# Where the modulation slabs stand in the weight stream of a three-block network

## The chip, the cores and the metric

The kernel runs on one core of one Trainium2 chip. The metric is the device time of one execution in microseconds, the lower the better.

## The reference

A sequence of 256 tokens of width 1024 goes through two layers and a third block. Each layer is an FFN, a mixer and another FFN; a vector `m` that is computed from the condition `c` shifts and scales the input of each of them and gates its output:

```python
cond = jax.nn.silu(c)
for l in range(DEPTH):
    m = (cond @ w_mod[l] + b_mod[l]).reshape(bsz, 3, 3, D_MODEL)
    x = x + 0.5 * m[:, 0, 2][:, None] * swiglu(adaln_in(x, norm_g[l, 0], m, 0), ...)
    h = adaln_in(x, norm_g[l, 1], m, 1) @ w_in[l]
    mix = mixer_ab(h, ...) if l % 2 == 0 else mixer_cd(h, ...)
    x = x + m[:, 1, 2][:, None] * (mix @ w_out[l])
    x = x + 0.5 * m[:, 2, 2][:, None] * swiglu(adaln_in(x, norm_g[l, 2], m, 2), ...)
```

`w_mod[l]` has 1024 x 9216 numbers, nine sections of 1024 columns for each layer: a shift, a scale and a gate for each of the three sublayers. mixer_ab is windowed attention beside a short gated convolution, mixer_cd is dense attention beside a long convolution by a Fourier transform. The third block has a hybrid mixer (a gated linear recurrence and latent attention), attention to a memory, and a convolved FFN; it has no modulation. All data are float32.

## The kernel before, in words

**Two kinds of slabs.** All large weights lie in memory as 417 weight slabs (`wst`) of 128 x 1024 float32, 512 KB each, in the order in which the matmuls need them. `w_mod` lies there as 144 modulation slabs (`mst`) of the same size. Both kinds go through one ring of six buffers in SBUF, `raws` (line 528), and one list, `order` (lines 552 to 561), says in what sequence. `load_job` issues one transfer after the other on SyncE's queue (line 572), each as soon as a buffer of the ring is free.

**What happens to a weight slab.** ScalarE copies it to a rounded type (`hi_job`, line 594), and VectorE subtracts that copy from the slab (`lo_job`, line 608); this gives a pair in the ring `hlr` of five pairs. Both are called its conversions. TensorE multiplies each 128 x 128 block of a pair with the input, also split in two, in three matmuls of 256 or 258 columns (`mm3`), so that the accuracy of float32 is kept. A slab holds eight blocks, 24 matmuls.

**What happens to a modulation slab.** It holds 128 columns of `w_mod`, with the 1024 inputs along the free dimension. VectorE multiplies it with the condition and sums the products, in one instruction (lines 619 to 621, `tensor_tensor_reduce`, with a read of the accumulator behind it). This is called a reduction here. `lo_job` takes the slabs of both kinds in the order of the list, so a reduction stands in the same queue as VectorE's conversions. Four of the 144 slabs go to TensorE instead (`pe_mod`). Of the last section of a sublayer all eight slabs must be done before the sublayer can use it: the shift of the second FFN of a layer for instance is needed at that FFN's first matmuls.

**What the list's sequence is.** Sixteen modulation slabs stand at the start, twelve of them ahead of the first weight slab. Then `RATES` (line 304) gives for each stretch of weight slabs how many modulation slabs follow one weight slab on average: its pairs are the number of the weight slab at which a stretch ends, and the rate.

```python
    credit += next(r for e, r in RATES if i < e)
    while credit >= 1.0 and mi < NM:
        order.append(("m", mi))
```

**The stages, by weight slab.** First layer: FFN 0 to 42 up projection, 43 to 64 down projection; mixer_ab 65 to 82 in-projection, 83 to 90 out-projection; second FFN 91 to 133 up, 134 to 155 down. Second layer: FFN 156 to 198 up, 199 to 220 down; mixer_cd 221 to 238 in-projection, 239 to 246 out-projection; second FFN 247 to 289 up, 290 to 311 down. Third block: hybrid mixer 312 to 342, attention to the memory 343 to 350, FFN 351 to 416.

**How the rest is ordered.** The program is written as some hundreds of small coroutines ("jobs"). A list scheduler (`Sched`, lines 335 to 431) runs them against a rough cost of each instruction and always takes the job that could start first on its engine, so the order on every engine is fixed when the program is built. Another list of slabs makes it order the whole program anew. All engine instructions are recorded through one helper, so the profile shows them at one line, 445.

**The start of a sublayer.** The squares of the new `x` are summed, a matmul with a column of ones gives the row sums, VectorE takes the reciprocal root of them in a chain of small operations (`rsqrt`, `TENSOR_SCALAR` and so on of 128x2), TensorE spreads it over the partitions and ScalarE copies the result (`Norm.root`, `spread`). Only then can the results of a slab's matmuls be scaled (`evict`), which gives their bank of PSUM back; there are three such banks (`mmr`), so TensorE can do three slabs' worth of up-projection matmuls before it needs the first of them again. In the layers' FFNs and mixers the shift is two more columns of the input (258 instead of 256).

**The ends of the mixers.** The out-projection multiplies the mixer's outputs with `w_out`. The last outputs are split in two on ScalarE and VectorE as the input is (`split`), and the out-projection's first sums wait for them: in mixer_ab for the last channel block of the convolution, in mixer_cd for the long convolution.

Of the kernel before, what the change touches and what calls it, by code (L numbers as in the profile page):

```python
# [300 lines left out]

PHASE = 8

RATES = [(43, 0.55), (65, 0.7), (91, 0.5), (156, 0.31), (199, 0.5), (221, 0.75), (247, 0.4), (10 ** 6, 0.2)]
STAGES = (65, 91, 156, 221, 247, 312, 343, 351)

TUNE = {}
# [169 lines left out]
def _body(tc, ins, out, ctx, dbg=None):  # L477
# [76 lines left out]
    for i in range(NW):  # L554
        if i:
            order.append(("w", i))
        credit += next(r for e, r in RATES if i < e)
        while credit >= 1.0 and mi < NM:
# [1786 lines left out]
```

## Time and profile before

| what | us |
|---|---|
| three timed runs | 1431.0, 1426.72, 1430.66 |
| median | 1430.66 |
| profiled execution, whole | 1425.9 |
| its span, first to last instruction | 1424.0 |
| TensorE busy | 1375.6 |
| VectorE busy | 1141.8 |
| ScalarE busy | 778.2 |
| mean granted clock of TensorE | 0.984 |

The profile shows one execution. Its span is 1.9 us shorter than that execution's own time, and this execution is 4.8 us faster than the median of the timed runs. Times in the trace's views count from the span's start. TensorE's clock has two levels, 2.4 GHz (1.00 in the column PEclk) and 1.2 GHz; a window that shows about 0.5 was at the lower one throughout. By the trace the stages begin about here: FFN 55, mixer_ab 248, its out-projection 328, second FFN 354 (down projection 481), second layer's FFN 543 (down projection 669), mixer_cd 730, its out-projection 814, second FFN 851, hybrid mixer 1049, attention to the memory 1190, last FFN 1232.

In the timeline rows the first number is the start, the second the time until the group's last instruction ends, `x` the number of instructions, and the bracket the engine's idle time before the group and the engine whose result ended it. `CUSTOM_DVE_ANT_0` of 128x1024 is a reduction, `TENSOR_TENSOR` of 128x1024 is VectorE's conversion.

### The profile page before, as it was taken

What the parts mean: (1) busy time and instruction counts of PE and PEld (TensorE: products, weight loads), DVE (VectorE), ACT (ScalarE), POOL (GpSimd) and SP (SyncE); (2) the same over time, 40 slices, a digit from 0 to 9 for tenths busy, and PEclk for the clock granted to TensorE, in tenths of its full rate; (3) what the DMA queues carried; (4) which work ended last, traced back from release to release, by engine and by line L of the source; (5) the groups of instructions that cost most, each with busy time, mean ns of one, the idle gap of its engine ahead of it and who ended that gap; (6) DMA issues with size and microseconds to landing.
All of it is one profiled execution on the core that took longest, in us unless ns stands there. A gap on an engine that the chain in (4) does not pass through costs nothing.

```text
span 1424.0 us, 26962 instructions
## 1 busy us (share of the span) xinstructions
PE 1375.6 (97%) x10726; PEld 1292.5 (91%) x10726; DVE 1141.8 (80%) x2183; ACT 778.2 (55%) x1434; POOL 40.9 (3%) x44
## 2 busy tenths in 40 slices
PE   5899999999999999999999999999999999999998
PEld 1499999878999999999998789999998779899998
DVE  5788788796888777888979879986577878799962
ACT  2365554474555544555447646655455765576642
POOL 5200000000000000000000001000000000000000
PEclk9999999999999999999999999999998999899999
DMA  8678889754787776888974447676643244366671
GB/s 296 220 252 315 290 311 326 241 160 152 248 264 249 239 246 226 299 272 279 343 283 152 158 146 231 221 253 184 192 143 107 72 130 138 90 184 186 193 228 54
DMA packets 84655, 305.25 MB, mean 214 GB/s; under 512 B 9515, under 2 KB 11147, under 8 KB 84274
## 3 DMA queue, kind: packets, MB, share of 16 engines
q1 hardware_dynamic: 83250, 299.31, 64.5%
q0 software_dynamic: 1280, 4.22, 0.9%
q8 instruction: 84, 1.38, 0.4%
q14 instruction: 41, 0.34, 0.1%
HBM read 302.43 MB, written 1.06 MB: 213 GB/s over the span
## 4 chain that ended last, share of the span: by engine, by line
PE 84%; DVE 7%; ACT 5%; DMA 1%; POOL 1%; issue 1%; SPq 0%; ACTq 0%; DVEq 0%; POOLq 0%
PE u L445 84%; DVE u L445 7%; ACT u L445 4%; POOL u L445 1%; DMA u<-wst 1%; DMA u<-x 1%; ACT L445 0%; SPq L572 0%; POOL u L2151 0%; ACTq L445 0%; DVEq L445 0%; DVE u L1655 0%; DVE u L1159 0%; DVE u L1656 0%; DVEq L1159 0%
## 5 line engine op out<-in xcount | busy, mean ns | idle before, releaser
L445 PE MATMUL u<-u,u 128*128 128x258 f32 (+7 forms) x10724 | 1374.5, 292 | 44.7 <-ACT u L445 24.2
L445 PEld LDWEIGHTS u<-u,u 128*128 128x128 f32 (+3 forms) x10724 | 1292.2, 189 | 126.1 <-issue 50.3
L445 ACT ACTIVATE u<-u 128x1024 fp32r<-128x1024 f32 (+6 forms) x1001 | 603.1, 632 | 534.0 <-PE u L445 311.3
L445 DVE TENSOR_TENSOR u<-u,u 128x1024 fp32r<-128x1024 f32 (+5 forms) x1065 | 734.0, 721 | 181.0 <-ACT u L445 91.9
L445 DVE SCALAR_TENSOR_TENSOR u<-u,u,u 128x256 f32<-128x256 f32 (+2 forms) x393 | 185.6, 481 | 65.2 <-PE u L445 34.2
L445 ACT ACTIVATE u<-u,u 128x256 f32<-128x256 f32 (+2 forms) x323 | 165.3, 523 | 85.6 <-DVE u L445 61.0
L445 DVE CUSTOM_DVE_ANT_0 u<-u,u,u 128x1024 f32<-128x1024 f32 x140 | 179.9, 1287 | 3.8 <-DMA u<-mst 3.7
L445 DVE SCALAR_TENSOR_TENSOR u<-u,u 128x2 f32<-128x2 f32 (+5 forms) x127 | 32.5, 261 | 13.3 <-ACT u L445 5.6
L445 ACT ACTIVATE u<-u,u,u 128x256 f32<-128x256 f32 (+1 forms) x43 | 23.8, 564 | 8.3 <-DVE u L445 5.7
L445 DVE TENSOR_SCALAR u<-u,u 128x256 f32<-128x256 f32 (+1 forms) x80 | 25.8, 370 | 1.6 <-ACT u L445 0.8
L445 DVE TENSOR_SCALAR u<-u 128x2 f32<-128x2 f32 (+9 forms) x82 | 14.9, 184 | 7.2 <-PE u L445 3.7
L445 POOL TENSOR_TENSOR u<-u,u 128x256 f32<-128x256 f32 (+1 forms) x10 | 14.5, 1448 | 12.3 <-ACT u L445 11.9
L445 DVE TENSOR_REDUCE u<-u 128x2 f32<-128x512 f32 x20 | 13.3, 683 | 1.9 <-PE u L445 1.9
L445 ACT ACT_TABLE_LOAD x11 | 14.1, 1283 | 0.9 <-PEq L2322 0.7
L1338 POOL DMA_DIRECT2D u<-rope x1 | 0.5, 548 | 480.0 <-PE u L445 480.0
L445 POOL TENSOR_SCALAR u<-u 64x256 f32<-64x256 f32 (+2 forms) x12 | 12.7, 1055 | 24.5 <-DVE u L445 18.4
L445 DVE DVE_READ_ACCUMULATOR2_ANT u<- 128x1 f32 x156 | 12.7, 82 | 0.0
L445 ACT ACTIVATION_READ_ACCUMULATOR u<-u,u,u 128x1 f32 x40 | 8.2, 205 | 0.0
L445 DVE TENSOR_TENSOR u<-u 128x2 f32<-128x2 f32 (+5 forms) x36 | 6.7, 189 | 0.6
L1153 POOL DMA_DIRECT2D u<-sel x1 | 0.6, 578 | 192.9 <-DMA u<-mst 192.9
L445 DVE CUSTOM_DVE_ANT_0 u<-u,u 128x256 f32<-128x256 f32 x16 | 6.0, 420 | 0.0
L445 DVE TENSOR_TENSOR_SCAN u<-u,u 128x256 f32<-128x256 f32 x8 | 5.4, 680 | 0.0
(35 smaller groups left out, 25.8 us busy)
## 6 DMA issues: line engine op xcount, KB each, us to landing
u<-wst SPq DMA_DIRECT2D x417, 512.0 KB, 4.5
u<-mst SPq DMA_DIRECT2D x144, 512.0 KB, 4.8
u<-u POOLq DMA_DIRECT2D x1, 1536.0 KB, 10.8
u<-x SPq DMA_DIRECT2D x1, 1024.0 KB, 8.2
u<-mem SPq DMA_DIRECT2D x1, 1024.0 KB
u<-lruw POOLq DMA_DIRECT2D x2, 512.0 KB, 4.3
out<-u SPq DMA_DIRECT2D x8, 128.0 KB, 3.3
u<-decay SPq DMA_DIRECT2D x1, 512.0 KB, 8.3
```

The lines of the kernel that those rows point to most:

```text
L445: r = f(*args, **kw)
L1153: nc.gpsimd.dma_start(sel, ins["sel6"][:8, :4 * P])
L1338: nc.gpsimd.dma_start(rope, ins["rope"])
```

## The change

`RATES` gets new numbers and more stretches. In the two in-projections (65 to 82 and 221 to 238) the rate is now 0.

```diff
-RATES = [(43, 0.55), (65, 0.7), (91, 0.5), (156, 0.31), (199, 0.5), (221, 0.75), (247, 0.4), (10 ** 6, 0.2)]
+
+RATES = [(43, 0.63), (65, 0.75), (83, 0.0), (91, 0.6), (134, 0.42), (156, 0.7), (199, 0.45), (221, 0.75), (239, 0.0),
+         (247, 0.3), (10 ** 6, 0.2)]
```

Modulation slabs in each stretch of weight slabs:

| weight slabs | stage | before | changed |
|---|---|---|---|
| 0 to 42 | FFN, up | 23 | 27 |
| 43 to 64 | FFN, down | 16 | 16 |
| 65 to 82 | mixer_ab, in | 9 | 0 |
| 83 to 90 | mixer_ab, out | 4 | 5 |
| 91 to 133 | second FFN, up | 13 | 18 |
| 134 to 155 | second FFN, down | 7 | 15 |
| 156 to 198 | second layer, FFN, up | 21 | 20 |
| 199 to 220 | FFN, down | 17 | 16 |
| 221 to 238 | mixer_cd, in | 7 | 0 |
| 239 to 246 | mixer_cd, out | 3 | 3 |
| 247 to 289 | second FFN, up | 8 | 8 |

The last modulation slab follows weight slab 283 before and 286 now. The last slab that the second FFN of the first layer needs at its start follows weight slab 82 before and 90 now; that FFN begins with weight slab 91.

How the orders differ is shown at three places. In the rows, numbers behind `u_` name buffers: `u_75` to `u_80` are the ring `raws`, `u_81` to `u_90` the pairs of `hlr` (the even ones are written by VectorE), `u_70` holds the modulation of the first layer, `u_142` the condition, `u_127` to `u_134` are the banks of PSUM, `u_67` is `x`. A reduction is two rows, `ISA u_7n,u_70<-...` and the read of its accumulator, `ISA u_70 128x1`. The line numbers of the changed file are larger by two.

VectorE at the end of mixer_ab: the last convolution (`u_91`), the split of it (`TENSOR_TENSOR u_2378<-u_91` or `u_2384<-u_91`, for which TensorE waits) and the conversion of weight slab 87 (`u_86`). Before:

```order
L445 SCALAR_TENSOR_TENSOR u_91<-u_2396,u_64,u_91 128x256
L445 SCALAR_TENSOR_TENSOR u_121<-u_70,u_63 128x8
L445 SCALAR_TENSOR_TENSOR u_91<-u_95,u_119,u_91 128x256
L445 ISA u_77,u_70<-u_77,u_142,u_63 128x1024
L445 ISA u_70 128x1
L445 TENSOR_TENSOR u_2378<-u_91,u_2377 128x256
L445 TENSOR_TENSOR u_86<-u_78,u_85 128x1024
```

Changed:

```order
L447 SCALAR_TENSOR_TENSOR u_91<-u_2402,u_64,u_91 128x256
L447 SCALAR_TENSOR_TENSOR u_121<-u_70,u_63 128x8
L447 SCALAR_TENSOR_TENSOR u_91<-u_95,u_119,u_91 128x256
L447 TENSOR_TENSOR u_86<-u_75,u_85 128x1024
L447 TENSOR_TENSOR u_2384<-u_91,u_2383 128x256
L447 ISA u_79,u_70<-u_79,u_142,u_63 128x1024
L447 ISA u_70 128x1
```

The conversion of slab 87 has moved ahead of the split, and the reduction behind it.

VectorE at the entry of the first layer's second FFN: the conversions of weight slabs 93 and 94 (`u_88` and `u_90`), the chain of the reciprocal root (from the `TENSOR_SCALAR` that reads bank `u_134`) and the reductions near them. Before:

```order
L445 TENSOR_TENSOR u_88<-u_79,u_87 128x1024
L445 TENSOR_TENSOR u_92<-u_92,u_101 128x256
L445 TENSOR_TENSOR u_90<-u_80,u_89 128x1024
L445 TENSOR_SCALAR u_103<-u_134 128x2
L445 TENSOR_SCALAR u_126<-u_103 128x2
L445 TENSOR_TENSOR u_122<-u_126 128x2
L445 TENSOR_TENSOR u_122<-u_122,u_103 128x2
L445 SCALAR_TENSOR_TENSOR u_103<-u_122 128x2
L445 SCALAR_TENSOR_TENSOR u_103<-u_103,u_122 128x2 x2
L445 SCALAR_TENSOR_TENSOR u_126<-u_103,u_126 128x2
L445 ISA u_76,u_70<-u_76,u_142,u_63 128x1024
L445 ISA u_70 128x1
```

Changed:

```order
L447 SCALAR_TENSOR_TENSOR u_69<-u_67,u_121,u_68 128x256
L447 ISA u_76,u_70<-u_76,u_142,u_63 128x1024
L447 ISA u_70 128x1
L447 TENSOR_TENSOR u_88<-u_77,u_87 128x1024
L447 TENSOR_TENSOR u_90<-u_78,u_89 128x1024
L447 TENSOR_TENSOR u_92<-u_92,u_100 128x256
L447 ISA u_75,u_70<-u_75,u_142,u_63 128x1024
L447 ISA u_70 128x1
L447 TENSOR_SCALAR u_123<-u_134 128x2
L447 TENSOR_SCALAR u_122<-u_123 128x2
L447 TENSOR_TENSOR u_124<-u_122 128x2
L447 TENSOR_TENSOR u_124<-u_124,u_123 128x2
```

Before, one reduction stands behind the chain. Now two stand ahead of it, and none directly behind it (the next row after the chain is the conversion of slab 95).

TensorE in the hybrid mixer: the query roots (`u_66` against squares in `u_91` to `u_102`, 128x8, twelve of them), rotations (`u_10868,u_66`), scores of the attention (`u_10882,u_10881`) and between them the matmuls of a slab (`u_127` to `u_129`). Before, from the ninth of the query roots on:

```order
L445 MATMUL u_131<-u_66,u_102 128x8
L445 MATMUL u_131<-u_66,u_94 128x8
L445 MATMUL u_131<-u_66,u_92 128x8
L445 MATMUL u_131<-u_66,u_98 128x8
L445 MATMUL u_128<-u_68,u_87 128x256
L445 MATMUL u_128<-u_69,u_87 128x256
L445 MATMUL u_128<-u_68,u_88 128x256
L445 MATMUL u_133<-u_10868,u_66 128x256
L445 MATMUL u_128<-u_68,u_87 128x256
L445 MATMUL u_128<-u_69,u_87 128x256
L445 MATMUL u_128<-u_68,u_88 128x256
L445 MATMUL u_130<-u_10869,u_66 128x256
```

Changed, up to the first two of them:

```order
L447 MATMUL u_129<-u_10895,u_85 128x256
L447 MATMUL u_129<-u_10896,u_85 128x256
L447 MATMUL u_129<-u_10895,u_86 128x256
L447 MATMUL u_130<-u_10868,u_66 128x256
L447 MATMUL u_129<-u_10895,u_85 128x256
L447 MATMUL u_129<-u_10896,u_85 128x256
L447 MATMUL u_129<-u_10895,u_86 128x256
L447 MATMUL u_131<-u_10882,u_10881 128x256 x2
L447 MATMUL u_128<-u_68,u_87 128x256
L447 MATMUL u_128<-u_69,u_87 128x256
L447 MATMUL u_128<-u_68,u_88 128x256
L447 MATMUL u_133<-u_66,u_100 128x8
```

The query roots stood ahead of the first of these rotations and now stand behind it and behind the first scores. Elsewhere in this stage rows have changed places in the same manner; their number is the same.

## Rows read from the trace of the kernel before

**Rows 1.** The page: its first line, and its line of busy times.
```profile
span 1424.0 us, 26962 instructions
...
PE 1375.6 (97%) x10726; PEld 1292.5 (91%) x10726; DVE 1141.8 (80%) x2183; ACT 778.2 (55%) x1434; POOL 40.9 (3%) x44
```

**Rows 2.** Windows by stage: window, its length, busy time of PE, PEld, DVE, ACT, POOL; PEclk, DMA share, GB/s.
```profile
247.70:327.50 79.80, 77.84 (x579) 66.19 (x578) 66.40 (x182) 45.48 (x114) 2.08 (x3) 1.00 0.63 202
...
354.10:481.20 127.10, 124.75 (x1042) 124.33 (x1041) 107.26 (x176) 70.68 (x132) 0.00 (x0) 1.00 0.77 249
...
481.20:542.80 61.60, 61.60 (x523) 61.60 (x522) 44.84 (x63) 30.54 (x42) 0.00 (x0) 1.00 0.78 248
...
668.50:730.00 61.50, 61.50 (x522) 61.50 (x521) 55.47 (x81) 30.55 (x42) 0.00 (x0) 1.00 0.93 330
...
730.00:814.20 84.20, 81.78 (x599) 69.56 (x599) 72.07 (x179) 54.72 (x122) 1.60 (x3) 1.00 0.53 177
```

**Rows 3.** Windows: a full FFN stretch, one FFN's start, three stretches at low clock.
```profile
680.00:720.00 40.00, 40.00 (x341) 40.00 (x340) 36.50 (x53) 19.44 (x25) 0.00 (x0) 1.00 0.96 342
...
332.20:335.60 3.40, 3.40 (x19) 3.40 (x18) 0.00 (x0) 0.00 (x0) 0.00 (x0) 0.53 0.78 263
...
354.00:359.00 5.00, 3.07 (x26) 2.86 (x25) 5.00 (x12) 2.58 (x5) 0.00 (x0) 1.00 0.70 203
...
827.10:830.50 3.40, 3.40 (x12) 2.81 (x11) 1.03 (x3) 0.42 (x1) 0.00 (x0) 0.54 0.38 143
...
1089.90:1100.20 10.30, 10.30 (x28) 6.85 (x29) 4.08 (x14) 0.67 (x2) 0.00 (x0) 0.51 0.18 51
```

**Rows 4.** The page's groups of instructions: the reductions of the modulation slabs.
```profile
L445 DVE CUSTOM_DVE_ANT_0 u<-u,u,u 128x1024 f32<-128x1024 f32 x140 | 179.9, 1287 | 3.8 <-DMA u<-mst 3.7
```

**Rows 5.** Timeline of TensorE, holes in brackets: mixer_ab (four rows), mixer_cd (three).
```profile
312.47 0.65 PE L445 MATMUL u<-u,u 128*64 128x256 f32 x2 [0.49 <-ACT u L445]
...
313.40 1.31 PE L445 MATMUL u<-u,u 128*64 128x256 f32 x6 [0.29 <-ACT u L445]
...
329.97 0.39 PE L445 MATMUL u<-u,u 128*128 128x256 f32 x1 [1.05 <-ACT u L445]
...
331.06 1.83 PE L445 MATMUL u<-u,u 128*128 128x256 f32 x12 [0.71 <-DVE u L445]
...
780.66 7.86 PE L445 MATMUL u<-u,u 128*128 128x128 f32 x54 [0.56 <-ACT u L445]
...
789.31 1.40 PE L445 MATMUL u<-u,u 128*128 128x128 f32 x10 [0.80 <-ACT u L445]
...
826.15 5.13 PE L445 MATMUL u<-u,u 128*128 128x256 f32 x16 [1.77 <-ACT u L445]
```

**Rows 6.** Timeline of VectorE: the ends of mixer_ab and mixer_cd (two rows each).
```profile
329.38 1.28 DVE L445 CUSTOM_DVE_ANT_0 u<-u,u,u 128x1024 f32<-128x1024 f32 x1
...
330.58 1.55 DVE L445 TENSOR_TENSOR u<-u,u 128x256 fp32r<-128x256 f32 x2
...
823.57 1.22 DVE L445 TENSOR_TENSOR u<-u,u 128x1024 fp32r<-128x1024 f32 x1
...
824.71 0.48 DVE L445 SCALAR_TENSOR_TENSOR u<-u,u,u 128x256 f32<-128x256 f32 x1
```

**Rows 7.** Timeline of VectorE, then TensorE: entry of the first layer's second FFN.
```profile
361.39 0.36 DVE L445 TENSOR_SCALAR u<-u 128x2 f32<-128x2 f32 x2
...
362.84 1.28 DVE L445 CUSTOM_DVE_ANT_0 u<-u,u,u 128x1024 f32<-128x1024 f32 x1
...
364.05 1.22 DVE L445 TENSOR_TENSOR u<-u,u 128x1024 fp32r<-128x1024 f32 x1
...
365.65 1.09 DVE L445 TENSOR_TENSOR u<-u,u 128x256 f32<-128x256 f32 x3 [0.39 <-PE u L445]
...
356.57 9.70 PE L445 MATMUL u<-u,u 128*128 128x258 f32 x79 [1.93 <-DVE u L445]
...
366.69 5.54 PE L445 MATMUL u<-u,u 128*128 128x258 f32 x44 [0.42 <-ACT u L445]
```

## The prediction

> **What bounds the kernel now.** First the page's busy times: TensorE is busy in 1375.6 of 1424.0 us, VectorE in 1141.8 [rows 1]. The kernel is a stream of matmuls, and only what shortens that stream or opens a hole in it moves the time. A share over the whole span does not tell what VectorE's work is worth in one stage, so the windows by stage come next [rows 2]. In the FFN stages TensorE works without a break: in the down projection of the first layer's second FFN (481.2 to 542.8) it is busy 61.60 of 61.60 us, with VectorE at 44.84. In the down projection after that (668.5 to 730.0) it is again busy 61.50 of 61.50, although VectorE is at 55.47 and the transfers at 0.93 of the DMA engines. In the in-projections of the two mixers TensorE is busy 77.84 of 79.80 and 81.78 of 84.20 us, VectorE 66.40 and 72.07. Third, the timeline of TensorE in the mixers gives every place where it stood: four small holes in the middle (0.49, 0.29, 0.56, 0.80, in all 2.14 us) and one hole at the end of each in-projection, 1.05 + 0.71 us in mixer_ab and 1.77 us in mixer_cd, in all 3.53 us [rows 5]. Behind each of those two end holes the granted clock is about 0.53 for 3.40 us, the lower of the two levels (1.2 instead of 2.4 GHz) [rows 3]; the lost half of such a stretch is 3.40 x 0.47 = 1.6 us, so 3.2 for both. Everything that a freer VectorE could give back in the mixers is therefore at most 2.14 + 3.53 + 3.2 = 8.9 us, 0.6% of the run.
>
> **What is taken out and what is put in.** The new rates take 9 modulation slabs out of the in-projection of mixer_ab and 7 out of that of mixer_cd; they put 4 more into the first FFN's up projection, 5 and 8 into the up and down projections of the first layer's second FFN, and one or two either way elsewhere. The number of slabs, transfers and reductions stays. On SP's queue the 17 weight slabs that follow the first of mixer_ab are now issued one after the other; the DMA engines are at 0.63 and 0.53 there [rows 2], so no transfer was late that could now come earlier. POOL issues none of them. One modulation slab costs VectorE one reduction of 1287 ns [rows 4]; from its start to the start of what follows it is 1.21 us (362.84 to 364.05, its read of the accumulator included) [rows 7]. So 9 x 1.21 = 10.9 and 7 x 1.21 = 8.5 us of VectorE's work leave the in-projections. That is cover time, not path: what counts are the holes.
>
> **FFN streams: 0.** The fullest FFN stretch after the change takes one slab in at 0.70 per weight slab (it was 0.31 there). The trace of before already has a stretch at 0.75: from 680 to 720 us TensorE is busy 40.00 of 40.00 us with VectorE at 36.50 and the DMA engines at 0.96, 342 GB/s [rows 3]. By work, 8 more reductions bring the stretch from 481.2 to 542.8 to 44.84 + 8 x 1.21 = 54.5 us, still below the 55.47 that the other one carries without a hole [rows 2]. In the up projection from 354.1 to 481.2, 5 more make 107.26 + 6.1 = 113.3 of 127.1. The cover is the spare ring of converted weights; if it were gone, each slab would cost its 1.21 us, but nothing in these windows says that it is near.
>
> **Middle of the mixers: -1.1.** The four holes of 2.14 us [rows 5] all end with ScalarE, which has no work of the modulation itself; VectorE's reductions can only delay what ScalarE waits for. Between all of it (-2.14) and none of it (0) I take half, as nothing in the rows places a reduction in each of these chains.
>
> **Ends of the mixers: -0.1.** Here the order decides. In mixer_ab the hole of 0.71 us waits for a split of the last convolution's output on VectorE, which starts at 330.58, behind a reduction that started at 329.38 [rows 6]. In the changed order the reduction stands behind the split, but the conversion of the next weight slab has moved ahead of it in its place. A conversion takes 1.14 to 1.2 us from start to start (823.57 to 824.71) where the reduction took 1.20 [rows 6], so some 0.1 us is gained. In mixer_cd the reduction and the conversion ahead of the last output stand in the changed order too, in the other sequence: 0. The bounds are 0 and the whole 3.53 us, with the 3.2 us of clock; I stay near 0 because the rows of the order are plain.
>
> **Entry of the second FFN: +1.8.** The first reciprocal root of that FFN is computed on VectorE (a chain of small operations, 361.39 to 362.84), and the results of the first three weight slabs can be scaled, and their PSUM banks given back, only behind it. TensorE fills those banks from 356.57 to 366.27 and then stands 0.42 us until 366.69 [rows 7]. Before, two conversions stand ahead of the chain and one reduction right behind it. In the changed order two reductions stand ahead of the chain and none directly behind. That is 2 x 1.21 = 2.4 us later for the chain. Of this the reduction that has gone from behind the chain gives back at most 1.21 and at least nothing: before the first scaling at 365.65 VectorE had idled already 0.39 us [rows 7], so it was not the reduction alone that held it. So the cost lies between 1.2 and 2.4 us; I take 1.8. The same entry in the other FFNs has no reduction ahead of the chain that was not hidden already, and costs nothing. The hole would become 0.4 + 1.8 = 2.2 us, in the size of the 1.77 us behind which the clock fell, but also of the 1.93 us at 356.57 [rows 7] behind which the clock stayed at 1.00 [rows 3]. One more fall would cost 1.6 us, which the range holds.
>
> **The rest: 0.** The list scheduler lays the whole program anew, so the hybrid mixer, which holds no modulation slab, is in another order too. The matmuls are the same in number; the price is unknown, and I take 0 with bounds from the neighbouring row: from 1089.9 to 1100.2 the clock is 0.51 for 10.30 us, that is 5.0 us lost [rows 3]. One such stretch more or less is -5 or +5.
>
> **Sum.** -1.1 - 0.1 + 1.8 + 0 = +0.6 us. On the profiled execution's 1425.9 us (the span of 1424.0 and 1.9 around it) this makes 1426.5. The three timed runs have a median of 1430.66, 4.8 above the profiled one; the same on the new sum gives **1431.3 us**. A measurement of this kernel tells about 0.3%, 4.3 us, from no change, so my forecast is no change.
>
> **Rivals.**
> *The mixers are VectorE's (faster).* If the end holes and all middle holes go, and the clock with them stays up, the gain is the whole 8.9 us, less 1.8 at the second FFN: 1430.7 - 7.1 = 1423.6. For it: VectorE is busy 72.07 of 84.20 us in mixer_cd, and 8.5 us of that leave. Against it: TensorE stands there for less than 2% of the time, and the end holes keep an operation of the same length ahead. The Trainium skill (Perfetto Trace Analysis, Identifying the Most-Contended Engine) says that matmul busy time is a bad measure and that the busy time of weight loads should be used. By it the mixers look open: weight loads are busy 66.19 of 79.80 and 69.56 of 84.20 us [rows 2], no more than VectorE, and the rival would be likely. I hold against it that a record of TensorE's hole, not its load queue, shows a wait, and that the holes add up to 5.7 us only. Chance 0.18.
>
> *The hybrid mixer loses a half-speed stretch (faster).* Its order changes: the small matmuls of the query roots move behind the first rows that they had preceded. If the stretch from 1089.9 goes, the time is 1431.3 - 5.0 = 1426.3. Nothing but the changed order speaks for it. Chance 0.08.
>
> *The hybrid mixer gains one (slower).* The same new order may leave TensorE with one more stretch of thin matmuls (one column group of 8 each) around which the clock falls for 10.30 us: 1431.3 + 5.0 = 1436.3. It decides from one added stretch on; a short one of 3.40 us (+1.6) leaves the time within 0.3%. For it: the stage has its own long stretch already, and its TensorE work is thin. Against it: the number of these matmuls is unchanged. The Trainium skill (TensorE: Matmul & The Clock Gate, What's actually happening) says that the throttled state is the default and that activity releases it; by it a stage with thin work is where an added fall is to be looked for. The trace agrees as far as it goes: the 10.30 us at 0.51 hold only 28 matmuls [rows 3]. Chance 0.20.
>
> *The change does not do what it says.* The in-projections hold no modulation slab any more, but the out-projections still take 5 and 3, and those stand next to the end holes. If what matters are only those, the time stays where it was, 1430.7. Chance 0.08; it is no change as well.
>
> **The numbers.** Forecast 0.46, change without effect 0.08: no change 0.54. Faster 0.18 + 0.08 = 0.26, slower 0.20. The range reaches from 1421.5 (the first rival without the 1.8 us at the second FFN, 1421.8) to 1437 (the slower rival, 1436.3).
>
> **What would show it.** Right: the hole in front of the fourth weight slab of the second FFN (before at 366.69) grows to about 2 us; the hole before the last output of both mixers is still over 1 us and the clock still falls behind it; the windows of both FFN down projections show TensorE busy without a break. Wrong: end holes below 0.5 us and the mixers' windows shorter by 3 us or more each (first rival), a hybrid mixer that is longer or shorter by 3 us or more (the others), or TensorE idle in the down projection of the second FFN.

## The result and the profile after

| | before | changed |
|---|---|---|
| median of four runs each, same chip | 1428.69 | 1448.69 |
| lowest and highest | 1424.42, 1431.0 | 1444.15, 1450.22 |
| ratio, 95% interval | | 1.014 [1.0114, 1.0166] |
| profiled execution: span | 1424.0 | 1442.4 |
| its mean granted clock | 0.984 | 0.974 |

The change makes the kernel slower by 20 us. The forecast was no change, and the time lies above the range. The page of the changed kernel, with the first line, the line of busy times and the clock by slices:

```profile
span 1442.4 us, 26979 instructions
...
PE 1386.9 (96%) x10726; PEld 1299.0 (90%) x10726; DVE 1146.1 (79%) x2183; ACT 778.0 (54%) x1434; POOL 39.3 (3%) x44
...
PEclk9899999899999999999999999999997899999999
```

The numbers of matmuls, of VectorE's and of ScalarE's instructions are those of before [rows 1]; TensorE is busy 11.3 us longer with the same work, and idle 7.1 us longer. More busy time for the same matmuls is time at the lower clock.

To place the 18.4 us, the time of the first matmul of each weight slab was taken in both traces and the difference followed along the program. It grows at four places and shrinks at one:

| stretch of weight slabs | grows by, us |
|---|---|
| mixer_ab, 65 to 91 | +4.75 |
| entry of the first layer's second FFN, 91 to 94 | +0.56 |
| mixer_cd, 221 to 247 | -1.77 |
| entry of the second layer's second FFN, 247 to 250 | +8.83 |
| hybrid mixer, 312 to 343 | +6.08 |
| all the rest, the FFN streams among it | 0.0 |

The windows of the changed kernel, in the columns of [rows 2]:

```profile
247.93:331.50 83.57, 82.15 (x578) 69.06 (x577) 58.41 (x168) 45.40 (x114) 2.08 (x3) 0.94 0.44 139
...
278.05:288.29 10.24, 10.24 (x38) 6.72 (x38) 4.49 (x19) 0.41 (x1) 0.00 (x0) 0.50 0.17 53
...
486.75:548.30 61.55, 61.55 (x523) 61.55 (x521) 55.10 (x81) 30.23 (x41) 0.00 (x0) 1.00 0.94 323
...
735.60:818.70 83.10, 81.33 (x599) 69.28 (x597) 66.25 (x167) 54.38 (x123) 1.61 (x3) 1.00 0.40 131
...
861.73:868.56 6.83, 4.60 (x21) 4.60 (x22) 5.40 (x18) 0.51 (x1) 0.00 (x0) 0.50 0.25 86
...
1051.30:1208.80 157.50, 152.48 (x968) 126.26 (x968) 120.86 (x313) 92.39 (x186) 1.66 (x3) 0.90 0.33 103
...
1097.25:1107.49 10.24, 10.24 (x30) 7.27 (x30) 6.08 (x12) 3.68 (x7) 0.00 (x0) 0.50 0.16 52
...
1110.90:1131.38 20.48, 20.48 (x76) 13.49 (x75) 17.14 (x44) 5.60 (x10) 0.00 (x0) 0.50 0.16 51
```

The in-projections hold no modulation slab any more, as the diff says: VectorE is busy 58.41 instead of 66.40 us in mixer_ab's in-projection and 66.25 instead of 72.07 in mixer_cd's, and the down projection that took eight slabs more runs without a break, 61.55 of 61.55 us [rows 2]. But mixer_ab has got a half-speed stretch of 10.24 us that was not there, in which the profile shows TensorE busy without a gap; that is 10.24 x 0.50 = 5.1 us. The hybrid mixer, with the same 968 matmuls, has two long half-speed stretches, 10.24 and 20.48 us, where before it had one of 10.30 [rows 3]. Its window of before, for comparison:

```profile
1038.90:1190.30 151.40, 145.99 (x968) 123.57 (x967) 120.25 (x316) 93.56 (x188) 1.66 (x3) 0.93 0.35 108
```

Over the whole stage the clock cost 151.40 x 0.07 = 10.6 us before and 157.50 x 0.10 = 15.8 us now, so 5.2 of the 6.08 us are clock.

The largest single piece is the entry of the second layer's second FFN. The timeline of the changed kernel there, VectorE (four rows), TensorE (three) and POOL (one):

```profile
855.29 0.16 DVE L447 TENSOR_TENSOR u<-u,u 128x16 fp32r<-128x16 f32 x1
...
862.88 0.29 DVE L447 CAST u<-u 128x256 f32<-128x256 int32 x1 [7.43 <-issue]
...
864.08 1.22 DVE L447 TENSOR_TENSOR u<-u,u 128x1024 fp32r<-128x1024 f32 x1
...
865.22 0.36 DVE L447 TENSOR_SCALAR u<-u 128x2 f32<-128x2 f32 x2
...
855.51 1.94 PE L447 MATMUL u<-u,u 128*128 128x258 f32 x14 [0.60 <-DVE u L447]
...
863.96 10.10 PE L447 MATMUL u<-u,u 128*128 128x1 f32 x65 [6.51 <-DVE u L447]
...
874.48 1.71 PE L447 MATMUL u<-u,u 128*128 128x258 f32 x12 [0.42 <-ACT u L447]
...
855.09 0.54 POOL L2166 DMA_DIRECT2D u<-pos  x1 [117.45 <-DVE u L447]
```

VectorE stands 7.43 us in front of a CAST. This instruction turns the token positions into floats, for the rotation tables of the hybrid mixer (the job `tables`, line 2169 of the changed file), and nothing in this FFN needs it. "issue" means that the view names no releaser. The chain of waits shows the same stretch:

```profile
855.09 0.28 DMA u<-pos
855.37 0.08 DVE u L447
855.45 7.43 issue
862.88 1.03 DVE u L447 x3
```

The releaser is found by adding: POOL issues the transfer of the positions at 855.09, and the list of DMA issues gives the time until it has landed as its last number:

```profile
u<-pos POOLq DMA_DIRECT2D x1, 128.0 KB, 7.7
```

855.09 + 7.7 = 862.79, and the CAST starts at 862.88. Behind it on VectorE are queued the conversions that feed TensorE (864.08) and the chain of the root (865.22), so TensorE stands 6.51 us and the clock is at half speed for 6.83 us. The timeline of the kernel before at this entry, VectorE and POOL:

```profile
858.06 0.55 DVE L445 SCALAR_TENSOR_TENSOR u<-u,u 128x2 f32<-128x2 f32 x3
858.55 0.29 DVE L445 CAST u<-u 128x256 f32<-128x256 int32 x1
...
850.77 0.54 POOL L2164 DMA_DIRECT2D u<-pos  x1 [118.43 <-PE u L445]
```

There the same CAST stood behind the conversions, the chain of the root and a reduction. The list of DMA issues of before gives this transfer 6.3 us:

```profile
u<-pos POOLq DMA_DIRECT2D x1, 128.0 KB, 6.3
```

So the positions were there at 850.77 + 6.3 = 857.07, and the CAST, at 858.55, waited for nothing. The scheduler gives POOL's transfers no duration in its cost model, so the two places look alike to it.

### The profile page after: what moved, and what is told of

It reads as the page before. It is cut to its first block, busy times and chain, and to the rows that moved or that the text cites. A ratio compares the mean times of both kernels' runs of the same rounds, so it can differ in the third digit from the quotient of the medians.

```text
span 1442.4 us, 26979 instructions
## 1 busy us (share of the span) xinstructions
PE 1386.9 (96%) x10726; PEld 1299.0 (90%) x10726; DVE 1146.1 (79%) x2183; ACT 778.0 (54%) x1434; POOL 39.3 (3%) x44
## 4 chain that ended last, share of the span: by engine, by line
PE 86%; DVE 6%; ACT 3%; issue 1%; DMA 1%; POOL 1%; SPq 0%; ACTq 0%; DVEq 0%; POOLq 0%
PE u L447 86%; DVE u L447 6%; ACT u L447 3%; POOL u L447 1%; DMA u<-wst 1%; DMA u<-x 1%; SPq L574 0%; ACT L447 0%; POOL u L2153 0%; DMA u<-pos 0%; ACTq L447 0%; DVEq L447 0%; DVE u L1657 0%; DVE u L1161 0%; DVE u L1658 0%
## 5 line engine op out<-in xcount | busy, mean ns | idle before, releaser
L447 PE MATMUL u<-u,u 128*128 128x256 f32 (+6 forms) x10724 | 1385.9, 294 | 51.8 <-ACT u L447 28.7
L447 PEld LDWEIGHTS u<-u,u 128*128 128x128 f32 (+2 forms) x10724 | 1298.7, 190 | 138.0 <-issue 57.5
L447 ACT ACTIVATE u<-u 128x1024 fp32r<-128x1024 f32 (+5 forms) x1001 | 604.6, 632 | 566.3 <-PE u L447 348.8
L447 DVE TENSOR_TENSOR u<-u,u 128x1024 fp32r<-128x1024 f32 (+4 forms) x1065 | 736.4, 722 | 183.1 <-ACT u L447 90.1
L447 ACT ACTIVATE u<-u,u,u 128x256 f32<-128x256 f32 (+1 forms) x43 | 23.9, 566 | 7.9 <-DVE u L447 6.4
L447 DVE RECIPROCAL u<-u 128x4 f32<-128x4 f32 (+2 forms) x17 | 3.0, 175 | 5.0 <-ACT u L447 4.7
(35 smaller groups left out, 28.8 us busy)
```

Source lines behind the costliest of these rows:

```text
L447: r = f(*args, **kw)
```

## The experiments

The theory after this reading: it is not the slabs' places that cost, but the order in which the list scheduler laid the rest anew. The rival: the slabs themselves (more reductions elsewhere, other lulls in VectorE's work) bring the loss. To part the two, the scheduler's choice was replaced by a recorded list of jobs. Only the reductions still go by the scheduler's rule, ahead of the next job of the list where their key is lower. All experiments but after_2 contain this:

```diff
 def run(self, main):
...
-            j = best[1]
+            nxt = next((j for j in self.ready if pos < len(SEQ) and j.key == SEQ[pos] and not self.is_mod(j)), None)
+            if nxt is not None:
+                if mod is not None and self.key_of(mod) < self.key_of(nxt):
+                    j = mod
+                else:
+                    j = nxt
+                    pos += 1
```

In the diffs below `order_of` is such a recorded list, and the other names say how it was edited; the kernels hold the finished lists. Each was timed beside the kernel before (64 runs over the three calls, median 1426.83, 1418.57 to 1433.85). "Lost" is the span times (1 - mean granted clock), averaged over the runs; it is about what the lower clock cost, since a stretch at half speed loses half its length where TensorE is busy all through it. "Rest" is the mean time without it, that is work at full speed and waits.

| kernel | median (runs) | ratio, 95% interval | lost | rest |
|---|---|---|---|---|
| before | 1426.83 (64) | | 25.3 | 1402.1 |
| changed, with after_2 | 1447.3 (10) | 1.014 and 1.013 | 38.5 | 1408.6 |
| move_only | 1422.12 (10) | 0.9979 [0.9951, 1.0006] | 25.7 with the next | 1400.4 with the next |
| move_only_2 | 1429.32 (12) | 1.0004 [0.9981, 1.0028] | | |
| order_only | 1439.96 (4) | 1.0085 [1.006, 1.011] | 28.8 | 1410.8 |
| cast_later | 1436.52 (7) | 1.007 [1.0046, 1.0093] | 30.8 | 1406.0 |
| ab_old_order | 1443.4 (5) | 1.0093 [1.0055, 1.0132] | 31.1 | 1410.5 |
| hybrid_old_order | 1439.29 (4) | 1.0077 [1.005, 1.0105] | 33.1 | 1406.3 |
| both_apart | 1430.0 (12) | 1.0013 [0.9996, 1.0031] | 22.5 | 1407.0 |
| after_mended | 1432.6 (10) | 1.0038 [1.0016, 1.0059] | 25.1 | 1408.6 |
| positions_early | 1436.53 (7) | 1.0075 [1.0045, 1.0105] | 33.9 | 1403.5 |
| hybrid_apart | 1426.47 (12) | 0.9992 [0.9966, 1.0017] | 23.2 | 1403.2 |

**The slabs alone: move_only.** The new rates, with the jobs in before's order; TensorE's and ScalarE's orders are then exactly those of before.

```diff
+SEQ = order_of(before)
```

> The new list of slabs, but every other job in the order of the kernel before: TensorE's, ScalarE's and POOL's instructions stand exactly as before, on VectorE only the reductions have moved. Theory (the re-sorted order costs the time, not the slabs' places): 1424 to 1432 us, TensorE's clock about 0.984, no wait of some 7 us at the start of the second layer's second FFN. Rival (the slabs themselves cost it, by work that the FFN stages cannot take): 1443 us or more, with TensorE idle in the FFN stages.

Measured: 0.9979 [0.9951, 1.0006]; the median lies 2 us below the range of the theory. The same slabs in the same places cost nothing. By slabs, its profile is 2.48 us shorter than before's in mixer_ab and 1.13 in mixer_cd, and the entries of the second FFNs are where they were. Of the 2.48 us 1.7 are a fall of the clock that before has behind the end of mixer_ab (332.2 to 335.6 [rows 3]) and this profile has not.

**The order alone: order_only.** The old rates, with the jobs in the changed kernel's order.

```diff
-RATES = [(43, 0.63), (65, 0.75), (83, 0.0), (91, 0.6), (134, 0.42), (156, 0.7), (199, 0.45), (221, 0.75), (239, 0.0),
-         (247, 0.3), (10 ** 6, 0.2)]
+RATES = [(43, 0.55), (65, 0.7), (91, 0.5), (156, 0.31), (199, 0.5), (221, 0.75), (247, 0.4), (10 ** 6, 0.2)]
+SEQ = order_of(changed)
```

> The old list of slabs, but every other job in the order of the changed kernel. Theory (order): 1443 to 1452 us, with the half-speed stretch in mixer_ab near 278 us, the wait of about 6.5 us near 864 us and some 30 us at half speed in the hybrid mixer. Rival (slabs): 1425 to 1432 us.

Measured: 1.0085 [1.006, 1.011], 1439.96 us, between the two ranges. The order without the change's slabs costs 0.9%, some six tenths of the loss. Its profile is 5.47 us longer in the hybrid mixer, but the entry costs only 2.83, because the positions landed after 4.2 us here and VectorE stood 1.95 us. Mixer_ab does not get the half-speed stretch near 278 us (it is 2.43 us longer all the same, with 6.83 us at half speed at its end where before had 3.41); the window there:

```profile
273.00:290.00 17.00, 17.00 (x114) 13.22 (x113) 13.54 (x49) 7.64 (x16) 0.00 (x0) 1.00 0.66 212
```

So the theory "order alone" holds for two of the three places, and some 7 us of the loss come only where the new order and the new slabs meet.

**The CAST moved back: cast_later.** The changed kernel with the job `tables` 60 places later.

```diff
-SEQ = order_of(changed)
+SEQ = moved_back(order_of(changed), "tables", 60)
```

> The changed kernel with the jobs of the rotation tables (first of them the cast of the positions) 60 places later in the order from the second layer's second FFN on; TensorE's order is untouched. Theory: the 6.5 us in which TensorE stands near 864 us is VectorE waiting for the positions' transfer, so it goes and the time falls by 6 to 9 us, to 1440 to 1443. Rival (the wait at that entry comes from the slabs or from the shift of the new FFN): the hole stays over 4 us and the time at 1446 to 1450.

Measured: 1.007, 1436.52 us, some 4 us below the range. The entry costs 2.42 instead of 8.83 us, and 1.53 more for a fall of the clock behind it. What remains is a neighbour in the list: the norm of the memory now stands ahead of the first scalings and waits for a transfer of 1 MB of its own, on ScalarE, for which VectorE then waits 3.87 us. ScalarE's row:

```profile
865.46 0.51 ACT L523 ACTIVATE u<-u,u 128x256 fp32r<-128x256 f32 x1 [7.59 <-DMA u<-mem]
```

The hybrid mixer too came out shorter here (+2.16), with the same matmuls in the same order, so the ratio alone does not show what the CAST is worth.

**mixer_ab in the old order: ab_old_order.** Only mixer_ab's jobs stand as before.

```diff
+SEQ = replaced(order_of(changed), "mixer_ab", order_of(before))
```

> The changed kernel with the jobs of mixer_ab in the order of before and all else in the changed order. Theory: the half-speed stretch of 10.24 us in mixer_ab comes from the closer packing of the small matmuls of the queries, so it goes and the time falls by 4 to 6 us, to 1443 to 1445. Rival (it comes from VectorE or the transfers with no slab in the mixer): the stretch stays, 1447 to 1450.

Measured: 1.0093, 1443.4 us. That number lies in the theory's range by luck: the half-speed stretch in mixer_ab is there all the same, and what was gained was gained elsewhere (the hybrid mixer is only 0.27 us longer than before's). The windows of ab_old_order and of move_only, which have mixer_ab in the same order:

```profile
277.44:291.10 13.66, 13.66 (x47) 8.79 (x46) 7.29 (x28) 1.72 (x3) 0.00 (x0) 0.50 0.15 57
```

```profile
273.45:282.30 8.85, 8.85 (x45) 5.28 (x45) 5.73 (x17) 2.22 (x4) 0.00 (x0) 1.00 0.36 113
```

TensorE is busy without a gap in both, and one runs at 0.50, the other at 1.00. The order within mixer_ab does not decide it. That theory falls. Up to the end of mixer_ab TensorE has the same matmuls in the same order in these two kernels, so the difference does not lie in TensorE's order at all; where it lies was not found.

**More slab matmuls between the small ones: both_apart.** What stands in the long ones of these stretches are matmuls with few rows of contraction (8 to 64 of 128), mostly with three full ones of a slab between them. This kernel is move_only with six instead of three in mixer_ab and the hybrid mixer.

```diff
+SEQ = spaced(order_of(before), ["mixer_ab", "hybrid_mixer"], 6)
```

> As move_only, but in mixer_ab the four spreads and first scores of the queries, and in the hybrid mixer the six spreads of the key roots and the first scores, have six matmuls of a weight slab between one and the next instead of three. Theory (the half-speed stretches follow small matmuls that stand too close): no half-speed stretch near 275 us in any run, the one of 10.24 us in the hybrid mixer (1084 to 1096) gone, 1413 to 1420 us, and no longer runs at both 1418 and 1430. Rival (the stretches come from somewhere else, or the later scores only open another hole): the clock as in move_only, 1420 to 1432.

Measured: 1.0013 [0.9996, 1.0031], 1430.0 us: the rival's range, 10 us above the theory's. Its windows in mixer_ab and in the hybrid mixer, at 1.00 and 0.95:

```profile
270.00:290.00 20.00, 20.00 (x137) 16.15 (x137) 12.04 (x47) 9.27 (x19) 0.00 (x0) 1.00 0.35 116
...
1075.00:1110.00 35.00, 34.89 (x216) 28.19 (x215) 23.64 (x68) 21.76 (x37) 0.00 (x0) 0.95 0.33 106
```

In this profile the clock stays up; hybrid_apart below shows that it need not. And the chains that the small matmuls belong to end later, and TensorE runs out of slab work before they do. The timeline of TensorE shows a new hole in mixer_ab (before, the largest in its middle was 0.49 us [rows 5]):

```profile
314.93 0.65 PE L523 MATMUL u<-u,u 128*64 128x256 f32 x2 [2.91 <-ACT u L523]
```

Lost falls by 2.8 us against before, which the scatter of the runs hardly tells from nothing; the rest grows by 4.9. What the clock gives is paid back in waits.

**All three mended: after_mended.** The changed kernel's order with `tables` and the memory's norm later and six slab matmuls in both places.

```diff
+SEQ = spaced(moved_back(order_of(changed), {"tables": 75, "memory_norm": 40}), ["mixer_ab", "hybrid_mixer"], 6)
```

> The changed kernel in its own order but for three places: the tables and the norm of the memory later at the entry of the second layer's second FFN, and six instead of three matmuls of a slab between the small matmuls of mixer_ab and of the hybrid mixer. Theory (these three places make up the loss of 20 us): 1424 to 1432 us, no hole over 3 us at that entry and less than 16 us lost to the low clock. Rival (the loss is spread over the program, or lies with the slabs): 1438 or more.

Measured: 1.0038 [1.0016, 1.0059], 1432.6 us, just above the theory's range. The entry costs 0.01 us, and lost is down to 25.1, before's level, but not below the 16 that the theory asked for. Mixer_ab keeps its clock where six profiles of the changed slabs and order had lost it:

```profile
277.00:290.00 13.00, 12.67 (x89) 10.07 (x89) 8.81 (x36) 6.49 (x21) 0.00 (x0) 1.00 0.14 46
```

It is still 1.99 us longer than before's, by a new hole of 1.94 us and a short fall. So about 14 of the 20 us go, and what stays is in the rest (1408.6 against 1402.1), as in both_apart.

**The hybrid mixer in the old order: hybrid_old_order.** The changed kernel up to there, then before's order.

```diff
+SEQ = until(order_of(changed), "hybrid_mixer") + since(order_of(before), "hybrid_mixer")
```

> The changed kernel, with the order of before from the hybrid mixer on. Theory (order): the hybrid mixer is 4 to 6 us shorter than in the changed kernel, 1442 to 1445 us, the hole near 864 us stays. Rival (the hybrid mixer is slow by the phase of the clock alone): as the changed kernel, 1447 to 1450, or spread over both.

Measured: 1.0077 against 1.014 and 1.013, by these ratios 8 to 9 us less; 1439.29 us is 3 us below the theory's range. In its profile the stage is 0.65 us shorter than before's and 6.7 shorter than the changed kernel's, the entry costs 8.98 us, and mixer_cd, which has the changed kernel's order, is at half speed for 10.24 us near 766 us, where no other profile of that order is. Of the half-speed stretches in the hybrid mixer one is long:

```profile
1110.30:1120.50 10.20, 10.20 (x29) 7.11 (x27) 5.09 (x14) 1.14 (x3) 0.00 (x0) 0.50 0.29 93
```

**A repeat of move_only: move_only_2.** Its first result was 0.2% below before, at the edge of its interval.

> The kernel of move_only once more, to tell its gain from the scatter. If moving the slabs alone pays: 1418 to 1424 in most runs and a ratio below 0.998 with its interval below 1. If it does not: ratio between 0.998 and 1.002. The profile shows a second time whether mixer_ab falls to half speed with the same order.

Measured: 1.0004 [0.9981, 1.0028]. No gain. Mixer_ab has no half-speed stretch in this profile either and is 2.41 us shorter than before's; mixer_cd is as long as before's (+0.07), with a half-speed stretch of 6.83 us near 761 us. The 22 runs together have a median of 1426.80 beside 1426.83, a lost share equal to before's and a rest that is 1.7 us lower.

**A repeat of the change: after_2**, beside the next kernel.

> The changed kernel once more, for its scatter. If the half-speed stretches of its first profile (mixer_ab, 20 us in the hybrid mixer) belong to its order, they stand in this profile too and the runs lie at 1444 to 1450. If they depend on where an execution's clock happens to stand, some of them are missing here and single runs reach 1435 or less. The wait of about 6.5 us for the positions stands in either case.

Measured: 1.013 [1.01, 1.016]. Both long stretches and the wait are there again. The hybrid mixer is at half speed even longer here, with the same program:

```profile
1101.95:1139.50 37.55, 37.55 (x136) 27.79 (x135) 25.67 (x62) 11.83 (x19) 0.00 (x0) 0.50 0.20 57
```

At the entry of the first layer's second FFN this profile shows what the first had not, a fall of the clock behind the hole (TensorE's row, then the window):

```profile
374.96 20.29 PE L447 MATMUL u<-u,u 128*128 128x258 f32 x155 [2.79 <-ACT u L447]
...
374.91:378.32 3.41, 3.36 (x15) 3.36 (x16) 2.80 (x4) 2.73 (x6) 0.00 (x0) 0.50 0.69 220
```

**The positions early: positions_early.** The changed kernel in its own order, the CAST where it was; only the transfer that it waits for is issued earlier, in mixer_cd, into a buffer that is free until the tables are made.

```diff
+    posi = rope2[:, 1].bitcast(I32)
...
+            nc.gpsimd.dma_start(posi, bass.AP(ins["pos"].tensor, ins["pos"].offset, [[0, P], [1, T]]))
...
-        posi = tl(sp, [P, T], I32)
-        nc.gpsimd.dma_start(posi, bass.AP(ins["pos"].tensor, ins["pos"].offset, [[0, P], [1, T]]))
```

> The changed kernel in its own order on every engine, but POOL issues the transfer of the positions in mixer_cd, over 100 us before VectorE's cast reads them. Theory (TensorE's hole near 864 us is the cast waiting for that transfer): the hole of 6.5 us goes, and the half-speed stretch of 6.83 us behind it with it, 8 to 10 us less than the changed kernel in the same call. Rival (VectorE is held there by the slabs or the shift): the hole stays.

Measured: 1436.53 beside 1445.95 for after_2 on the same chip, 9.4 us less (medians of 7 and 6 runs; by the means 9.1, with a 95% interval of about 4 to 14). The timeline of this kernel at the entry, VectorE, TensorE, POOL:

```profile
859.27 0.29 DVE L523 CAST u<-u 128x256 f32<-128x256 int32 x1
...
859.42 9.73 PE L523 MATMUL u<-u,u 128*128 128x258 f32 x79 [0.61 <-DVE u L523]
...
870.17 10.07 PE L523 MATMUL u<-u,u 128*128 128x258 f32 x82 [1.03 <-ACT u L523]
...
741.53 0.55 POOL L1421 DMA_DIRECT2D u<-pos  x1
```

The CAST stands in the same place and waits for nothing, the hole of 6.51 us is gone, and the entry takes 0.63 us more than before's instead of 8.83. This settles that the wait was for the positions' transfer. By slabs the entry is 8.0 us shorter than in after_2. The hybrid mixer of this profile is the worst of all:

```profile
1091.45:1132.41 40.96, 40.96 (x145) 29.75 (x144) 26.59 (x65) 12.51 (x20) 0.00 (x0) 0.50 0.19 59
```

**The hybrid mixer alone apart: hybrid_apart.** both_apart without its part in mixer_ab.

```diff
+SEQ = spaced(order_of(before), ["hybrid_mixer"], 6)
```

> As move_only, with six matmuls of a slab between the small matmuls of the hybrid mixer alone (in the kernel with both, mixer_ab had lost about 5 us and the hybrid mixer had gained about 2). If that holds: 2 us below move_only, 1421 to 1425, ratio 0.996 to 0.999. If the scatter of the clock made it: ratio 0.999 to 1.003.

Measured: 0.9992 [0.9966, 1.0017], 1426.47 us: the reading by scatter. Its hybrid mixer has the list of both_apart, job by job, and is 1.86 us longer than before's where that one was 1.77 shorter; a long half-speed stretch has come back a little later in the stage:

```profile
1122.85:1133.09 10.24, 9.76 (x36) 6.05 (x36) 8.46 (x20) 2.65 (x6) 0.00 (x0) 0.50 0.18 53
```

So six matmuls between the small ones do not hold the clock up there. Over the runs lost is some 2 us lower than before's, within their scatter, and the rest 1.1 higher; of both_apart's 4.9 us of waits, then, 3.8 come from mixer_ab. No version was found that beats the kernel before by more than its measurement can tell.

**The loss, put together.** By the means, 38.5 - 25.3 = 13.2 us of it are clock, and 1408.6 - 1402.1 = 6.5 us are waits; 5.1 of these go in positions_early (1403.5). By place:

- The CAST's wait with the fall behind it: 9.4 us. The cause is shown by positions_early.
- mixer_ab's half-speed stretch: the stage is 4.75 to 5.62 us longer. This is shown as a place, not as a cause: it fell in all six profiles that have the changed kernel's slabs, its order ahead of mixer_ab and three slab matmuls between the small ones, and in none of the others; which detail counts stays open.
- The hybrid mixer: some 5 us on average, with a wide scatter (table).
- The entry of the first layer's second FFN: 0.3 to 1.1 us, and 1.5 more for a fall of the clock behind its hole, in six of the seven profiles that have the change's slabs and order there. The first profile of the changed kernel is the seventh.
- Against it stand some 2 us that the slabs give back.

Growth of the hybrid mixer against the profile of before, and its time at half speed, for the order of its matmuls:

| order in the hybrid mixer | growth by profile, us | at half speed, us |
|---|---|---|
| before's: before, move_only, move_only_2, hybrid_old_order | 0, +0.08, +2.57, -0.65 | 20.5, 20.5, 23.9, 17.1 |
| changed: ab_old_order, cast_later, order_only, changed, after_2, positions_early | +0.27, +2.16, +5.47, +6.08, +9.14, +10.66 | 13.7, 20.5, 27.3, 30.7, 37.6, 44.4 |

With TensorE's order the same, the stage grows by anything from 0.3 to 10.7 us. The window of ab_old_order, to set beside the 157.50 us of the changed kernel:

```profile
1056.30:1208.00 151.70, 144.64 (x968) 121.84 (x968) 120.19 (x313) 92.82 (x186) 1.66 (x3) 0.95 0.35 107
```

The means are +5.6 for the changed order and +0.5 for before's, and hybrid_old_order's runs are 8 us faster than the changed kernel's, so the order counts. How far the clock falls within it is not settled by the order alone.

## Why the prediction was wrong, by its steps

**FFN streams, 0: right.** The down projection with eight more slabs runs 61.55 of 61.55 us, with VectorE at 55.10 where 54.5 was forecast.

**Entry of the first layer's second FFN, +1.8: the mechanism right, the sum of its parts not.** TensorE's timeline of the changed kernel there:

```profile
359.08 10.37 PE L447 MATMUL u<-u,u 128*128 128x258 f32 x80 [0.30 <-ACT u L447]
...
371.97 8.27 PE L447 MATMUL u<-u,u 128*128 128x258 f32 x67 [2.52 <-ACT u L447]
```

The hole in front of the fourth slab grew from 0.42 to 2.52 us (forecast 2.2). The hole at the shift ahead of it, which the sum had left as it was, shrank from 1.93 to 0.30 [rows 7]. The net is +0.56, and in this profile the clock did not fall. In the six others with these slabs and this order the hole is 2.4 to 2.8 us and the clock falls behind it, which makes 1.8 to 2.6 us in all. So a size like +1.8 is met there, but with two things that the sum had left out: the hole at the shift shrinks, and the clock falls.

**Ends of the mixers, -0.1: near. Middle, -1.1: right in size, by a guess between two bounds.** The same timeline at the ends (mixer_ab two rows, mixer_cd one), and the two middle holes that are left:

```profile
334.30 0.39 PE L447 MATMUL u<-u,u 128*128 128x256 f32 x1 [1.56 <-ACT u L447]
...
335.32 4.86 PE L447 MATMUL u<-u,u 128*128 128x256 f32 x26 [0.64 <-DVE u L447]
...
830.45 5.79 PE L447 MATMUL u<-u,u 128*128 128x256 f32 x19 [1.77 <-ACT u L447]
...
313.27 11.96 PE L447 MATMUL u<-u,u 128*64 128x256 f32 x88 [0.30 <-ACT u L447]
...
784.75 35.72 PE L447 MATMUL u<-u,u 128*128 128x128 f32 x237 [0.78 <-ACT u L447]
```

The end holes are still over 1 us, as forecast, 1.56 + 0.64 where 1.05 + 0.71 stood, 0.4 us more, and 1.77 unchanged. Of the 2.14 us in the middle 1.08 are left [rows 5]. The slabs alone (move_only and its repeat, 22 runs) give -1.7 us in the rest and no difference in time that can be measured; the forecast for these two terms was -1.2. So the rival by which the mixers are VectorE's was rightly set aside: 8 and 6 us less of VectorE's work there (10.9 and 8.5 were forecast) bought some 2 us. Two readings were off without harm: TensorE stood for 2.5 and 2.9% of the two in-projections, not less than 2% [rows 2], and the list of holes left out the two at the start of each mixer, 0.66 + 0.41 us in mixer_ab, which did not change.

**"The same entry in the other FFNs ... costs nothing": the step that failed first.** It asked only where the reductions stand. What matters at this entry is everything ahead of the conversions and the chain on VectorE, and there the re-laid order had put an instruction that belongs to a stage 190 us later and waits for a transfer just issued. Its price was 8.83 us in the profile and 9.4 by the runs of positions_early, where the sum had nothing. The row was to be had: the CAST of before at 858.55 stands 1.5 us behind the landing of its data, and the order shows it moved ahead of the chain.

**"The rest: 0", with bounds of 5 us: the step that failed second.** The list scheduler's new order was taken as neutral, with one stretch of 10.3 us either way as the most. Two stages lost clock: the hybrid mixer 5.2 us more than before, and mixer_ab 5.1 us, which no case held. The rival "the hybrid mixer gains one" was right in its kind and place and near in size for this profile (+5.0 for a stage that grew by 6.08, and by 9.14 in the repeat). That the size came so near is partly luck, as the same order gave 0.27 to 10.66 us, and it covered a third of the growth. Together with the entry this takes the time beyond the 1437 at which the range ended.

## What to carry to other kernels

Where a list scheduler lays the program, a change of its input is two changes: the one in the diff, and a new order of everything. Replaying a recorded order parts them: here the new places alone cost nothing, the new order alone 12 us, and the two together 20, so both halves have to be run. In the order, look for instructions that wait for a transfer and have moved ahead of work that feeds the bounding engine, and give the scheduler's model a duration for every transfer, or issue it long before.

## What the runs showed of the hardware

**The clock fell without any gap in TensorE's row.** From 278.05 to 288.29 TensorE is busy 10.24 of 10.24 us and the granted clock is 0.50; in the hybrid mixer the same holds for up to 40.96 us in one piece. The ends of matmuls are modelled in the profile, and the weight loads are busy 6.72 and 29.75 us in these two stretches, so a full row of matmuls is not an engine at its peak. What stands there are matmuls with few rows of contraction among full ones. That these are the reason is argued, not shown: with six full ones instead of three between them mixer_ab's place ran at 1.00 in after_mended, but in the hybrid mixer one and the same list with six was at half speed for 6.8 us once (both_apart) and for 17.1 us once (hybrid_apart), and the thin matmuls of mixer_ab ran at 1.00 with three between them in move_only. The Trainium skill (TensorE: Matmul & The Clock Gate, Why this matters for your kernels) advises to avoid idle gaps of TensorE between bursts of matmuls, for the clock's sake. These stretches hold no such gap, so a timeline without holes does not show that the clock stays up.

**The same program gets a different amount of it from run to run.** Before's 64 runs reach from 1418.57 to 1433.85 us; move_only ran once in 1417.6 us with a mean clock of 0.987 and once in 1430.3 with 0.978. 1420 x 0.009 = 12.8 us is about all of that difference. A change of this kernel that touches its clock has to be timed in many runs, and one profile shows one case of several.

**A transfer of 128 KB on POOL's queue took 4.2 to 9.5 us to land**, at the same place of the program (4.2 in order_only, 6.3 before, 7.7 changed, 9.5 in ab_old_order), beside large transfers on the other queue. The Trainium skill (DMA: Bandwidth & Descriptors, Anatomy of one DMA — SWDGE (gpsimd) path) fits a fixed 2.0 us and a term by size, which would make an estimated 2.3 us for 128 KB. The measured landings are longer and decide; a wait on such a transfer is to be planned by the longest of them.
